# Row-wise max-norm of an 8192 x 8192 matrix: an earlier table load, smaller GpSimd shares and another queue for the last store

## The chip, the cores and the metric

The kernel runs on one core of one Trainium2 chip. Its time is the device time of an execution in microseconds (us). The span in a profile is about 1.8 us shorter than the time of the same execution (627.7 against 629.47 us). Two per cent is 12.6 us.

## The reference

```python
def setup_inputs():
    return {"x": np.random.randn(8192, 8192).astype(np.float32)}

def reference(x):
    return np.linalg.norm(x, ord=np.inf, axis=1)
```

With `axis=1` this is the largest absolute value of each row: 268.4 MB are read, 32 KB are written.

## The kernel before

Rows go to the 128 partitions in 64 tiles of 128 rows. Two single-row tiles come first, then 30 tiles with two rows in each partition, then two single-row tiles, the last of them in five pieces. VectorE reduces nearly everything. In the last three tiles GpSimd takes a share g of the columns. Its reduction takes no absolute value in this kernel, so ScalarE takes that first, in place.

```python
TILES = (                      # pieces of each tile: (columns, columns of GpSimd's share)
    [[(8192, 0)]] * HEAD
    + [[(16384, 0)]] * (PAIRS - 1)
    + [[(16384, 7168)], [(8192, 3584)]]
    + [[(4160, 1792), (2048, 896), (1024, 448), (512, 0), (448, 0)]]
)
...
    def absmax_pool(dst, src):
        keep(nc.scalar.activation(src, src, mybir.ActivationFunctionType.Abs))   # L77
        max_pool(dst, src)                                                       # L66, GpSimd
...
            nc.sync.dma_start(out=buf, in_=src[:, off : off + w])                # L120
            off += w
            if final:
                pairs_out()                     # two transposes, copies and a store on ScalarE
                absmax(res[:, R - 1 :], last)   # L59: the last piece and the partial maxima
            elif u == len(TILES) - 1:
                ...                             # absmax and absmax_pool into columns of `last`
...
    ps_ones = psum_pool.tile([n_ones, P], FP32)
    sb_ones = single.tile([n_ones, P], FP32)
    nc.tensor.transpose(ps_ones, res[:, X_ONE:], ident)
    nc.vector.tensor_copy(out=sb_ones, in_=ps_ones)
    nc.sync.dma_start(out=out[X_ONE * P :].rearrange("(r p) -> r p", p=P), in_=sb_ones)
```

The ring holds three pair tiles; each load waits until VectorE has read what it overwrites (before: 29 such waits of SyncE, 490.8 us in all).

Of the kernel before, what the change touches and what calls it, by code (L numbers as in the profile page):

```python
# [1 line left out]

# [5 lines left out]

P = 128
FP32 = mybir.dt.float32  # L10
INT32 = mybir.dt.int32
MAX = mybir.AluOpType.max
X = mybir.AxisListType.X





HEAD = 2
PAIRS = 30  # L20
TILES = (
    [[(8192, 0)]] * HEAD
    + [[(16384, 0)]] * (PAIRS - 1)
    + [[(16384, 7168)], [(8192, 3584)]]
    + [[(4160, 1792), (2048, 896), (1024, 448), (512, 0), (448, 0)]]
)
RING = 3 * 16384


@with_exitstack  # L30
def kernel(
    ctx: ExitStack,
    tc: tile.TileContext,
    x: bass.AP,
    out: bass.AP,
):
    nc = tc.nc
    n_rows, n_cols = x.shape
    R = n_rows // P
    assert R == 64 and n_cols == 8192  # L40

    X_ONE = 2 * PAIRS
    n_ones = R - X_ONE
    keep = tc.keep_in_program_order

    single = ctx.enter_context(tc.tile_pool(name="single", bufs=1))
    psum_pool = ctx.enter_context(tc.tile_pool(name="psum", bufs=1, space=bass.MemoryType.PSUM))

    ring = single.tile([P, RING], FP32)
    res = single.tile([P, R], FP32)  # L50
    ident = single.tile([P, P], FP32)


    n_part_last = sum((w > g) + (g > 0) for w, g in TILES[-1][:-1])
    w_last = TILES[-1][-1][0]
    last = single.tile([P, w_last + n_part_last], FP32)

    def absmax(dst, src):
        return keep(nc.vector.tensor_reduce(  # L59
            out=dst, in_=src, axis=X, op=MAX, apply_absolute_value=True,  # L60
        )).ins

    def max_pool(dst, src):

        pool = nc.gpsimd
        keep(pool.add_instruction(  # L66
            mybir.InstTensorReduce(
                name=nc.get_next_instruction_name(),
                ins=[pool.lower_ap(src.bitcast(INT32))],
                outs=[pool.lower_ap(dst.bitcast(INT32))],  # L70
                op=MAX,
                axis=X,
            )
        ))

    def absmax_pool(dst, src):
        keep(nc.scalar.activation(src, src, mybir.ActivationFunctionType.Abs))  # L77
        max_pool(dst, src)

    def setup(after):  # L80

        tc.add_manual_dep(
            nc.gpsimd.memset(ident, 0.0).ins, after.name,  # L83
            mybir.DependencyInfo(mybir.DependencyClass.Sync, mybir.DependencyReason.DATA),
            reason="not before the first row is in",
        )
        make_identity(nc, ident, nomemset=True)

    def pairs_out():
        sb = single.tile([PAIRS, P, 2], FP32, name="sb_pairs")  # L90
        both = res[:, :X_ONE].rearrange("p (g r) -> p g r", r=2)
        for r in range(2):
            ps = psum_pool.tile([PAIRS, P], FP32, name=f"ps_pairs{r}")
            nc.tensor.transpose(ps, both[:, :, r], ident)  # L94
            keep(nc.scalar.copy(sb[:, :, r], ps))  # L95
        keep(nc.scalar.dma_start(
            out=out[: X_ONE * P].rearrange("(g p r) -> g p r", p=P, r=2), in_=sb
        ))

    at = 0  # L100
    next_pair, next_one = 0, X_ONE
    for u, pieces in enumerate(TILES):
        k = sum(w for w, _ in pieces) // n_cols
        if k == 2:
            row, next_pair = next_pair, next_pair + 2
        else:
            row, next_one = next_one, next_one + 1
        src = x[row * P : (row + k) * P].rearrange("(p r) m -> p (r m)", r=k)
        off = 0
        n_part = 0  # L110
        for h, (w, g) in enumerate(pieces):
            final = u == len(TILES) - 1 and h == len(pieces) - 1
            if final:
                buf = last[:, :w]
            else:
                if at + w > RING:
                    at = 0
                buf = ring[:, at : at + w]
                at += w
            nc.sync.dma_start(out=buf, in_=src[:, off : off + w])  # L120
            off += w
            if final:
                pairs_out()
                absmax(res[:, R - 1 :], last)
            elif u == len(TILES) - 1:
                for eng, a, e in ((absmax, 0, w - g), (absmax_pool, w - g, w)):
                    if a < e:
                        i = w_last + n_part
                        eng(last[:, i : i + 1], buf[:, a:e])
                        n_part += 1  # L130
            elif g == 0:
                red = absmax(
                    res[:, row : row + k], buf.rearrange("p (c m) -> p c m", m=n_cols)
                )
                if u == 0:
                    setup(red)
            else:

                part = single.tile([P, 2], FP32, name=f"part{u}")
                c = w // n_cols - 1  # L140
                if c:
                    absmax(res[:, row : row + c], buf[:, : c * n_cols])
                absmax(part[:, 0:1], buf[:, c * n_cols : w - g])
                absmax_pool(part[:, 1:2], buf[:, w - g :])
                max_pool(res[:, row + c : row + c + 1], part)

    ps_ones = psum_pool.tile([n_ones, P], FP32)
    sb_ones = single.tile([n_ones, P], FP32)
    nc.tensor.transpose(ps_ones, res[:, X_ONE:], ident)  # L149
    nc.vector.tensor_copy(out=sb_ones, in_=ps_ones)  # L150
    nc.sync.dma_start(out=out[X_ONE * P :].rearrange("(r p) -> r p", p=P), in_=sb_ones)


# [1 line left out]
_INS = ['x']  # L155
_OUTS = [((8192,), 'float32')]


# [23 lines left out]
```

## Time and profile before

| | before |
|---|---|
| time, median of 3 runs | 629.39 us (629.32 to 629.58) |
| span | 627.7 us |
| last pair tile landed | 603.52 us |
| last reduction starts | 624.00 us |
| last store is issued | 625.40 us |
| from that issue to the span's end | 2.30 us |

The page rounds a span to 0.1 us, which is too coarse for what follows; times from a moment to the span's end are taken from the trace files, which have it to 0.001 us. T0 is the start of the VectorE reduction that waits for the last two-row tile. Up to T0 the transfers set the pace: those of x take 99.0% of the span of the 16 DMA engines together, and VectorE idles 2.12 us before the reduction at T0. After it come 24.18 us in which the last tiles are reduced and written. I will count moments of the tail from T0, because T0 itself differs from run to run.

These are the entries of the program's closing line in SyncE's queue (min/median/max duration in ns, then the first and the last start in us):

```profile
L177 SPq EVENT_SEMAPHORE  x7: 17/28/28, 625.8 to 627.6; - x7
L177 SPq DRAIN  x3: 7/7/124, 626.7 to 627.4; - x3
```

One of the three drains takes 124 ns, where the others take 7, and it starts only at 627.4 us.

### The profile page before, as it was taken

How to read it: one execution, taken by the hardware profiler on the slowest of the kernel's cores; microseconds unless marked ns; L12 is line 12 of the kernel's file. 1: busy time of each engine (PE TensorE's matmuls, PEld its weight loads, DVE VectorE, ACT ScalarE, POOL GpSimd, SP SyncE). 2: the span in 40 equal slices, each digit the busy share in tenths (PEclk: the TensorE clock that was granted, in tenths of full speed). 3: DMA queues.
4: the chain of work that ended last, by engine and by line, in shares of the span. 5: the costliest groups of instructions: out<-in, count | busy, mean ns of one | idle time of the engine just before them, and what ended most of it. 6: DMA issues, size and time to landing. Idle time of an engine off the chain costs nothing.

```text
span 627.7 us, 194 instructions
## 1 busy us (share of the span) xinstructions
PE 1.1 (0%) x3; PEld 0.3 (0%) x3; DVE 537.5 (86%) x40; ACT 14.2 (2%) x8; POOL 13.4 (2%) x13
## 2 busy tenths in 40 slices
PE   0000000000000000000000000000000000000000
PEld 0000000000000000000000000000000000000000
DVE  1938988889988889888898888988889988889887
ACT  0000000000000000000000000000000000000044
POOL 0000000000000000000000000000000000000007
DMA  8999999999999999999999999999999999999996
GB/s 368 434 468 401 468 401 468 401 468 401 468 401 468 401 468 401 464 405 464 405 464 405 459 409 459 409 459 409 459 409 451 418 451 418 434 434 422 447 401 269
DMA packets 5525, 268.47 MB, mean 428 GB/s; under 512 B 627, under 2 KB 789, under 8 KB 1045
## 3 DMA queue, kind: packets, MB, share of 16 engines
q1 hardware_dynamic: 5480, 268.44, 99.0%
q10 hardware_dynamic: 45, 0.03, 0.0%
HBM read 268.44 MB, written 0.03 MB: 428 GB/s over the span
## 4 chain that ended last, share of the span: by engine, by line
DMA 70%; DVE 28%; issue 1%; POOL 1%; SPq 0%; POOLq 0%; PE 0%
DMA ring<-in_x_dram 70%; DVE res L59 28%; POOL part L66 0%; POOL last L66 0%; SPq L120 0%; POOLq L177 0%; PE ps_ones L149 0%; DVE sb_ones L150 0%; POOL res L66 0%; POOLq L66 0%
## 5 line engine op out<-in xcount | busy, mean ns | idle before, releaser
L59 DVE TENSOR_REDUCE res<-ring 128x2 f32<-128x16384 f32 (+1 forms) x32 | 525.4, 16420 | 86.8 <-DMA ring<-in_x_dram 86.8
L66 POOL TENSOR_REDUCE part<-ring 128x1 int32<-128x7168 int32 (+1 forms) x2 | 9.3, 4672 | 588.5 <-ACT ring L77 588.5
L77 ACT ACT_TABLE_LOAD x1 | 1.3, 1283 | 603.6 <-DMA ring<-in_x_dram 603.6
L77 ACT ACTIVATE ring<-ring 128x7168 f32<-128x7168 f32 (+4 forms) x5 | 12.6, 2518 | 5.2 <-DMA ring<-in_x_dram 2.9
L59 DVE TENSOR_REDUCE part<-ring 128x1 f32<-128x1024 f32 (+1 forms) x2 | 6.1, 3076 | 0.0
L59 DVE TENSOR_REDUCE last<-ring 128x1 f32<-128x2368 f32 (+3 forms) x4 | 5.2, 1348 | 0.0
L66 POOL TENSOR_REDUCE last<-ring 128x1 int32<-128x1792 int32 (+2 forms) x3 | 3.1, 1061 | 0.0
L94 PE MATMUL ps_pairs<-ident,res 128*30 128x128 f32 x2 | 0.8, 384 | 617.2 <-DVE res L59 612.3
L59 DVE TENSOR_REDUCE res<-last 128x1 f32<-128x455 f32 x1 | 0.6, 628 | 0.6 <-POOL last L66 0.6
L150 DVE COPY sb_ones<-ps_ones 4x128 f32<-4x128 f32 x1 | 0.3, 279 | 0.5 <-PE ps_ones L149 0.5
L83 POOL MEMSET ident<- 128x128 f32 x1 | 0.2, 205 | 21.6 <-DVE res L59 21.6
L94 PEld LDWEIGHTS ps_pairs<-ident,res 128*30 128x30 f32 x2 | 0.2, 106 | 617.5 <-issue 612.3
L95 ACT COPY sb_pairs<-ps_pairs 30x128 f32<-30x128 f32 x2 | 0.4, 254 | 0.0
L66 POOL TENSOR_REDUCE res<-part 128x1 int32<-128x2 int32 x2 | 0.4, 196 | 0.1
L149 PE MATMUL ps_ones<-ident,res 128*4 128x128 f32 x1 | 0.4, 372 | 6.7 <-DVE res L59 6.7
masks.py:199 POOL TENSOR_SCALAR_AFFINE_SELECT ident<-ident 128x128 f32<-128x128 f32 x1 | 0.3, 294 | 0.1
L166 POOL MEMSET const-float32-0.0<- 128x1 f32 x1 | 0.1, 99 | 0.2 <-issue 0.2
L166 POOL MEMSET const-bfloat16-1.0<- 128x1 bf16 x1 | 0.1, 102 | 0.0
L166 POOL MEMSET const-uint8-127<- 128x1 uint8 x1 | 0.1, 102 | 0.0
L166 POOL MEMSET const-float32-1.0<- 128x1 f32 x1 | 0.1, 99 | 0.0
L149 PEld LDWEIGHTS ps_ones<-ident,res 128*4 128x4 f32 x1 | 0.1, 81 | 7.0 <-DVE res L59 7.0
## 6 DMA issues: line engine op xcount, KB each, us to landing
ring<-in_x_dram SPq DMA_DIRECT2D x3, 4096.0 KB, 21.8
ring<-in_x_dram SPq DMA_DIRECT2D x1, 2080.0 KB, 35.7
ring<-in_x_dram SPq DMA_DIRECT2D x1, 1024.0 KB, 37.8
ring<-in_x_dram SPq DMA_DIRECT2D x1, 512.0 KB, 38.6
ring<-in_x_dram SPq DMA_DIRECT2D x30, 40.8
ring<-in_x_dram SPq DMA_DIRECT2D x1, 256.0 KB, 38.8
last<-in_x_dram SPq DMA_DIRECT2D x1, 224.0 KB, 38.8
out_dram<-sb_pairs ACTq DMA_DIRECT2D x1, 30.0 KB, 1.5
```

Of the source, the lines that this page charges most:

```text
L59: return keep(nc.vector.tensor_reduce(out=dst, in_=src, axis=X, op=MAX, apply_absolute_value=True,)).ins
L66: keep(pool.add_instruction(mybir.InstTensorReduce(name=nc.get_next_instruction_name(), ins=[pool.lower_ap(src.bitcast(INT32))], outs=[poo ...
L77: keep(nc.scalar.activation(src, src, mybir.ActivationFunctionType.Abs))
L83: nc.gpsimd.memset(ident, 0.0).ins, after.name,
L94: nc.tensor.transpose(ps, both[:, :, r], ident)
L95: keep(nc.scalar.copy(sb[:, :, r], ps))
L149: nc.tensor.transpose(ps_ones, res[:, X_ONE:], ident)
L150: nc.vector.tensor_copy(out=sb_ones, in_=ps_ones)
L166: nc = _bacc.Bacc("TRN2", target_bir_lowering=False, num_devices=1)
```

## The change

ScalarE loads its table while nothing waits for it; GpSimd gets fewer columns and the last tile is cut a little differently; ScalarE makes the last copy and issues the last store.

```diff
-    + [[(16384, 7168)], [(8192, 3584)]]
-    + [[(4160, 1792), (2048, 896), (1024, 448), (512, 0), (448, 0)]]
+    + [[(16384, 7168)], [(8192, 3328)]]
+    + [[(4160, 1760), (2080, 832), (1024, 384), (512, 0), (416, 0)]]
...
+    def load_table(after):
+        abs_ident = nc.scalar.activation(
+            ident[:, :1], ident[:, :1], mybir.ActivationFunctionType.Abs
+        )
+        tc.add_manual_dep(keep(abs_ident).ins, after.name, ...)
...
                 if u == 0:
                     setup(red)
+                elif u == 1:
+                    load_table(red)
...
-    nc.vector.tensor_copy(out=sb_ones, in_=ps_ones)
-    nc.sync.dma_start(out=out[X_ONE * P :].rearrange("(r p) -> r p", p=P), in_=sb_ones)
+    keep(nc.scalar.copy(sb_ones, ps_ones))
+    keep(nc.scalar.dma_start(
+        out=out[X_ONE * P :].rearrange("(r p) -> r p", p=P), in_=sb_ones
+    ))
```

Cut here: the two transposes of the pair rows move to an earlier place in the program; they still wait for the same data.

More of the change, by code (lines that the diff above doesn't have):

```diff
@@ L87, in setup, with transpose_pairs @@
         make_identity(nc, ident, nomemset=True)
+    def load_table(after):
+        abs_ident = nc.scalar.activation(
+            ident[:, :1], ident[:, :1], mybir.ActivationFunctionType.Abs
+        )
+        tc.add_manual_dep(
+            keep(abs_ident).ins, after.name,
+            mybir.DependencyInfo(mybir.DependencyClass.Sync, mybir.DependencyReason.DATA),
+            reason="not before the second row is in",
+        )
+    ps_pairs = [psum_pool.tile([PAIRS, P], FP32, name=f"ps_pairs{r}") for r in range(2)]
+    def transpose_pairs():
+        both = res[:, :X_ONE].rearrange("p (g r) -> p g r", r=2)
+        for r in range(2):
+            keep(nc.tensor.transpose(ps_pairs[r], both[:, :, r], ident))
     def pairs_out():
         sb = single.tile([PAIRS, P, 2], FP32, name="sb_pairs")
-        both = res[:, :X_ONE].rearrange("p (g r) -> p g r", r=2)
         for r in range(2):
-            ps = psum_pool.tile([PAIRS, P], FP32, name=f"ps_pairs{r}")
-            nc.tensor.transpose(ps, both[:, :, r], ident)
-            keep(nc.scalar.copy(sb[:, :, r], ps))
+            keep(nc.scalar.copy(sb[:, :, r], ps_pairs[r]))
         keep(nc.scalar.dma_start(
@@ L121 @@
             off += w
+            if u == len(TILES) - 1 and h == 0:
+                transpose_pairs()
             if final:
```

## The prediction

> **What bounds the kernel now.** I read the page's engine shares and its slices first. VectorE is busy 86% and nothing else computes before the last 25 us, but the transfers are busy in every slice:
>
> ```profile
> PE 1.1 (0%) x3; PEld 0.3 (0%) x3; DVE 537.5 (86%) x40; ACT 14.2 (2%) x8; POOL 13.4 (2%) x13
> ...
> DMA  8999999999999999999999999999999999999996
> ...
> q1 hardware_dynamic: 5480, 268.44, 99.0%
> ```
>
> The 268.44 MB of x occupy the 16 DMA engines for 99.0% of the span. VectorE takes 17.22 us for a pair tile and then idles 2.12 to 2.14 us for the next one. So the kernel is bound by the stream of x up to about 603 us, and the change leaves that stream as it is: same tiles, same order, same queue, and the same 8192 columns in the last row. What is in play is how long after the stream the program ends.
>
> I then read the chain that ended last, in order of time, from 611 us:
>
> ```profile
> 611.13 2.25 POOL part L66
> ...
> 620.90 1.16 POOL last L66
> 622.06 0.47 issue
> 622.52 0.94 POOL last L66
> 623.46 0.52 POOLq L177
> 623.98 0.02 issue
> 624.00 0.64 DVE res L59
> 624.64 0.04 issue
> 624.68 0.39 PE ps_ones L149
> 625.07 0.02 issue
> 625.09 0.28 DVE sb_ones L150
> ```
>
> The tail runs through GpSimd, then one VectorE reduction, a transpose, a copy and a store. The timeline says why GpSimd is late (columns: start us, duration us, engine, line, operation, count, and in brackets the idle time before it with what ended it):
>
> ```profile
> 603.52 8.69 DVE L59 TENSOR_REDUCE res<-ring 128x1 f32<-128x8192 f32 x1 [2.12 <-DMA ring<-in_x_dram]
> 603.59 1.28 ACT L77 ACT_TABLE_LOAD   x1 [603.59 <-DMA ring<-in_x_dram]
> 604.88 6.18 ACT L77 ACTIVATE ring<-ring 128x7168 f32<-128x7168 f32 x1
> 611.13 6.16 POOL L66 TENSOR_REDUCE part<-ring 128x1 int32<-128x7168 int32 x1 [588.52 <-ACT ring L77]
> 613.25 4.94 DVE L59 TENSOR_REDUCE part<-ring 128x1 f32<-128x4608 f32 x1
> 618.20 1.70 ACT L77 ACTIVATE ring<-ring 128x1792 f32<-128x1792 f32 x1 [1.73 <-DMA ring<-in_x_dram]
> 618.21 5.18 DVE L59 TENSOR_REDUCE last<-ring 128x1 f32<-128x2368 f32 x4
> 624.00 0.63 DVE L59 TENSOR_REDUCE res<-last 128x1 f32<-128x455 f32 x1 [0.61 <-POOL last L66]
> ```
>
> ScalarE gets its first data at about 603.5 us, spends 1.28 us on its table, and only then takes the absolute values that GpSimd needs. From 611.13 GpSimd runs with hardly a gap until 623.98. VectorE is just as unbroken: from 603.52 to 618.21 + 5.18 = 623.39. It then idles 0.61 us for GpSimd. **GpSimd holds the end by 0.61 us, and VectorE is right behind it.** The pieces themselves land at about 618.2, 620.7, 622.0, 622.7 and 623.1 us (issue plus time to landing; where ScalarE waits for them its starts agree), so data are the third bound.
>
> [...] The trace has 1283 ns exactly; the activation follows 1.29 us after the load started[...] and I count 1.28 us. [...] (8686 - 4944) ns / (8192 - 4608) = 1.044 ns an element, at every width. [...] VectorE's 8192 took 8.69 us alone at 23.00 us and 8.69 us beside the rest. So no second-order gain of VectorE from smaller GpSimd shares is counted. [...] No run yet shows the same store from both.
>
> **The change part by part.**
>
> *Table.* An Abs on one column of the identity after row tile 1 pulls the load to about 31.7 us, where ScalarE is idle. Adds one tiny activation off the path; removes 1.28 us before the 7168-wide Abs. Abs 603.60 to 609.78, GpSimd starts at 609.84 instead of 611.13.
>
> *GpSimd's chain.* Its cost is (6163 - 3182) ns / 3584 = 0.832 ns an element, ScalarE's (6176 - 3190) / 3584 = 0.833. GpSimd: 7168 to 616.00, combine to 616.24, 3328 (3.182 - 256 x 0.832 ns = 2.97 us) to about 619.4, combine to 619.6. Now it waits for ScalarE: Abs of 1760 from 618.20, 1.67 us, 619.87; GpSimd 1.66 us to 621.60. The 2080 piece lands 32 columns (16 KB, 0.04 us) later: Abs of 832 620.76 to 621.66, GpSimd 0.88 us to 622.60. Abs of 384 622.08 to 622.60, GpSimd 0.51 us to **623.16**, instead of 623.98. GpSimd becomes bound by landings and gains 0.82 us.
>
> *VectorE's chain.* It receives what GpSimd gives up: +256 columns (8192 piece), then +32, +96 and +64; the last reduction has 416 + 7 = 423 elements instead of 455. Successive reductions start 0.09 us before the former ends (618.21 to 620.74 for a 2.62 us one). 4864 wide: 4.944 + 0.267 = 5.21, from 613.25 to 618.46. 2400 wide: 2.65, from 618.37. 1248 wide: 1.44, from 620.94. 640 wide: 0.82, from 622.30. 512 wide: 0.68, from 623.04 to 623.71. So VectorE's pieces end 0.32 us later than before (623.39), and **VectorE takes over the end from GpSimd** with some 0.55 us to spare. The final reduction reads partial results that VectorE itself has just written; it has a semaphore wait of VectorE's queue ahead of it (0.233 us, begun at 623.2, ended about 0.04 us after the reduction before), so I don't let it overlap: it starts at about 623.77 and takes 0.628 - 32 x 1.044 ns = 0.595, ending at 624.37 against 624.63. Gain 0.26 us: 0.23 from the start, 0.03 from the width.
>
> *Transposes of the pairs.* Moved earlier in program order only. They waited for data (612.35 for VectorE, 617.62 for GpSimd's combine); the second now comes at about 616.3. Nobody on the path reads them. Zero.
>
> *Last copy and store.* The copy goes from VectorE (279 ns) to ScalarE (254 ns mean at 30x128): -0.03 us. The hand-over gains nothing: VectorE's copy ends at 625.37 and SyncE issues at 625.40; ScalarE's own copy to its own issue also took about 0.03 (622.93 to 622.96). The issue took 352 ns on SyncE for four partitions and 632 ns on ScalarE for thirty. After the issue's end both landed alike (1.5 - 0.63 = 0.87 and, by SyncE's wait that ended at 626.65, 1.25 - 0.35 = 0.90 us). I can't split 632 into the engine and the shape, so I put 0.40 on ScalarE: +0.05 us, and up to +0.28. ScalarE's queue is free by then (pairs' issue ends at 623.7).
>
> Sum: -0.26 - 0.03 + 0.05 = **-0.24 us**, so 629.39 - 0.24 = 629.15 us.
>
> **The rivals.** (a) *The saving on GpSimd is had in full:* 0.82 + 0.03 us, some 628.5. Against it: VectorE ended only 0.61 us earlier and receives 448 columns before the final reduction, so this needs work that VectorE can't hide. (b) *ScalarE's store eats it:* if every issue there costs 0.63 us the sum is about -0.01, 629.4. For it: the one issue seen there; against it: that one has 30 partitions. (c) *GpSimd still ends last:* would need a slip of over 0.55 us, for instance if its starts wait on something I don't see; then 629.2 to 629.5. (d) *The stream moves:* a table load or an Abs among the first tiles can't hold back a buffer, since the loads wait for VectorE's reductions and the earlier loads (SyncE's waits name only these), so I count nothing; but the stream's own scatter (runs 629.32 to 629.58) is as large as the effect.
>
> **Range and chances.** From -0.6 us (half way to (a), a lucky store) to +0.15 us (b plus scatter): 628.8 to 629.55. Two per cent are 12.6 us, while the whole tail after the stream, from 623.1 us to the span's end at 627.7, is 4.6 us. Removing it all would not be "faster", and nothing added is near 12 us. Faster 0.01, same 0.98, slower 0.01.
>
> **What would show it.** Right: the table load near 31.7 us; GpSimd's first big reduction at 609.8; the last reduction idle for VectorE's own result, not for GpSimd, with a start near 623.77 counted from the same landing of 603.5; GpSimd done 0.5 us before; the chain of waits with VectorE in place of GpSimd; ScalarE's last issue at 0.35 to 0.45 us. Wrong: a GpSimd wait left before the last reduction, a last issue of 0.6 us, or landings of the last pieces that moved by more than 0.1 us, which would mean the stream and not the tail made the difference.

The 1283 ns are the table load, and 1.044 ns an element is VectorE's reduction ((17220 - 8686) / 8192 and (8686 - 628) / (8192 - 455) both give 1.042). That smaller GpSimd shares bring VectorE no further gain rests on the two times of 8.69 us alone. The 0.04 us for 16 KB are an estimate; at the page's mean of 428 GB/s they come to 0.038.

## The result

The changed kernel took 628.66 us (median of 6 runs, 628.54 to 628.75), the kernel before beside it 629.36 us (629.15 to 629.63). The ratio is 0.9988, with a 95% interval from 0.9976 to 1.0001. A ratio is the mean time of one kernel's fast runs over that of the other's of the same rounds, so not quite the ratio of these medians. All outputs are right. The class (within 2%) was right, but the time fell below the predicted range of 628.8 to 629.55.

The timeline of the changed kernel, for the lines that were shown of before (start, duration, engine, line, operation, idle time before it and what ended it):

```profile
31.39 1.28 ACT L91 ACT_TABLE_LOAD   x1 [31.39 <-DVE res L59]
...
603.17 8.69 DVE L59 TENSOR_REDUCE res<-ring 128x1 f32<-128x8192 f32 x1 [2.14 <-DMA ring<-in_x_dram]
603.25 6.18 ACT L77 ACTIVATE ring<-ring 128x7168 f32<-128x7168 f32 x1 [570.36 <-DMA ring<-in_x_dram]
609.50 6.16 POOL L66 TENSOR_REDUCE part<-ring 128x1 int32<-128x7168 int32 x1 [587.26 <-ACT ring L77]
...
618.03 5.32 DVE L59 TENSOR_REDUCE last<-ring 128x1 f32<-128x2400 f32 x4
619.61 3.10 POOL L66 TENSOR_REDUCE last<-ring 128x1 int32<-128x1760 int32 x3 [0.39 <-ACT ring L77]
...
623.44 0.59 DVE L59 TENSOR_REDUCE res<-last 128x1 f32<-128x423 f32 x1
...
624.50 0.26 ACT L169 COPY sb_ones<-ps_ones 4x128 f32<-4x128 f32 x1 [2.06 <-PE ps_ones L168]
624.79 0.26 ACTq L170 DMA_DIRECT2D out_dram<-sb_ones  x1
```

The table load is out of the way (it takes 1.28 us from 31.39, and the activation behind it starts 1.30 us after it, at 32.69; before it was 1.29 us, 603.59 to 604.88), and GpSimd starts 6.33 us after T0 instead of 7.61. GpSimd is done at 619.61 + 3.10 = 622.71 us, VectorE's pieces only at 618.03 + 5.32 = 623.35. The last reduction no longer names a wait for GpSimd. The chain that ended last, in order of time, agrees: from T0 to the transpose it is VectorE alone.

```profile
603.17 8.69 DVE res L59
611.86 6.25 DVE part L59 x2
618.11 5.25 DVE last L59 x4
623.36 0.04 DVEq L59
623.39 0.05 issue
623.44 0.60 DVE res L59
```

From T0 the last reduction starts at 623.44 - 603.17 = 20.27 us (before: 20.48) and the last issue at 21.62 (before: 21.88). So the tail up to the issue is 0.26 us shorter. But from the issue to the span's end it is 2.00 us instead of 2.30. That is 0.30 us that the prediction did not have. The closing entries of SyncE's queue show a difference there; the late drain is gone:

```profile
L198 SPq EVENT_SEMAPHORE  x6: 17/28/28, 622.2 to 626.7; - x6
L198 SPq DRAIN  x3: 7/7/7, 626.0 to 626.3; - x3
```

The rest of the difference between the two profiles is T0 itself, 603.17 against 603.52 us, and it was there from the very first tile (landed at 12.92 against 13.30 us), where the two kernels do the same.

### The profile page after: what moved, and what is told of

Read it like the earlier page. It is cut to its first block, busy times and chain, and to the rows that moved or that the text cites. A ratio compares the mean times of both kernels' runs of the same rounds, so it can differ in the third digit from the quotient of the medians.

```text
span 626.8 us, 194 instructions
## 1 busy us (share of the span) xinstructions
PE 1.1 (0%) x3; PEld 0.3 (0%) x3; DVE 537.5 (86%) x39; ACT 14.3 (2%) x10; POOL 13.3 (2%) x13
## 4 chain that ended last, share of the span: by engine, by line
DMA 70%; DVE 29%; issue 0%; PE 0%; SPq 0%; ACT 0%; DVEq 0%
DMA ring<-in_x_dram 70%; DVE res L59 28%; DVE part L59 1%; DVE last L59 1%; PE ps_ones L168 0%; SPq L135 0%; ACT sb_ones L169 0%; DVEq L59 0%
## 5 line engine op out<-in xcount | busy, mean ns | idle before, releaser
L59 DVE TENSOR_REDUCE last<-ring 128x1 f32<-128x2400 f32 (+3 forms) x4 | 5.3, 1392 | 0.0
L66 POOL TENSOR_REDUCE last<-ring 128x1 int32<-128x1760 int32 (+2 forms) x3 | 3.0, 1016 | 0.5 <-ACT ring L77 0.4
L91 ACT ACT_TABLE_LOAD x1 | 1.3, 1283 | 31.4 <-DVE res L59 31.4
```

Of the source, the lines that this page charges most:

```text
L59: return keep(nc.vector.tensor_reduce(out=dst, in_=src, axis=X, op=MAX, apply_absolute_value=True,)).ins
L66: keep(pool.add_instruction(mybir.InstTensorReduce(name=nc.get_next_instruction_name(), ins=[pool.lower_ap(src.bitcast(INT32))], outs=[poo ...
L91: abs_ident = nc.scalar.activation(ident[:, :1], ident[:, :1], mybir.ActivationFunctionType.Abs)
```

## The experiments

The theory after the result had three terms: the tail up to the last issue, the end after it, and a scatter of T0. The rivals: the early table load makes the first tiles land sooner; or one part of the change carries all. Fourteen experiments ran, two of them repeats of the kernels before and after. All numbers of the tail come from one profile each, counted from that profile's T0. The last column is the median of all runs of the kernel in its batch.

| kernel | T0 | last reduction starts after T0 | last issue to end | T0 to end | time, median |
|---|---|---|---|---|---|
| before | 603.52 | 20.48 | 2.30 | 24.18 | 629.36 |
| before, again | 603.22 | 20.49 | 2.30 | 24.19 | 629.18 |
| table only | 603.10 | 19.92 | 2.30 | 23.62 | 628.71 |
| shares and recut only | 603.59 | 20.27 | 2.29 | 23.93 | 629.07 |
| copy and store only | 603.10 | 20.49 | 2.01 | 23.87 | 628.96 |
| changed | 603.17 | 20.27 | 2.00 | 23.62 | 628.66 |
| changed, again | 603.15 | 20.27 | 2.00 | 23.61 | 628.64 |
| changed, old shares | 603.25 | 19.92 | 2.00 | 23.31 | 628.27 |
| changed, old copy and store | 603.17 | 20.27 | 2.29 | 23.93 | 628.97 |
| changed, old store | 603.66 | 20.27 | 2.07 | 23.68 | 628.79 |
| changed, old copy | 603.21 | 20.28 | 2.00 | 23.65 | 628.76 |

Here the time less "T0 to end" lies between 604.96 and 605.18 us. So the tail explains most of the differences between the times, and some 0.2 us is scatter that it doesn't.

### One part at a time, on the kernel before

**Only the table.**

```diff
                 if u == 0:
                     setup(red)
+                elif u == 1:
+                    load_table(red)
```

> Only the early table load, on the kernel before. Theory (three separate terms: a tail term that either the table or the recut alone gives, a store term, and a first-landing term that is scatter): GpSimd's first big reduction starts 6.25 us after the last pair tile landed instead of 7.6, its pieces end near 623.2 on the old clock, VectorE's at 623.4 set the end, so the last reduction starts about 0.55 us sooner after that landing; time 0.5 us below before, some 628.85. First landing of x anywhere between 12.9 and 13.3 us. Rival (the early table load itself makes the first rows land sooner): first landing at 12.9 us again and 0.85 us below before, some 628.5.

628.71 us, ratio 0.9991 (0.9979 to 1.0004). The last reduction starts 0.56 us sooner after T0 than before: more than in the whole change. The timeline shows VectorE at its old pieces, without the wait for GpSimd:

```profile
617.78 5.14 DVE L59 TENSOR_REDUCE last<-ring 128x1 f32<-128x2368 f32 x4
...
619.55 3.22 POOL L66 TENSOR_REDUCE last<-ring 128x1 int32<-128x1792 int32 x3
...
623.02 0.63 DVE L59 TENSOR_REDUCE res<-last 128x1 f32<-128x455 f32 x1
```

**Only the shares and the recut.**

```diff
-    + [[(16384, 7168)], [(8192, 3584)]]
-    + [[(4160, 1792), (2048, 896), (1024, 448), (512, 0), (448, 0)]]
+    + [[(16384, 7168)], [(8192, 3328)]]
+    + [[(4160, 1760), (2080, 832), (1024, 384), (512, 0), (416, 0)]]
```

> Only the smaller GpSimd shares and recut last pieces. Theory: GpSimd ends near 623.55 and VectorE near 623.7 on the old clock, so the last reduction starts 0.2 us sooner after the landing of the last pair tile, and is 0.03 us shorter: the same 0.23 to 0.26 us that the whole change shows in its tail, without the table; time some 629.1. Rival (the table is what the tail gains from, the shares only follow): no gain here, 629.36.

629.07 us, ratio 0.9997 (0.9984 to 1.0009). The last reduction starts 20.27 us after T0, exactly as in the whole change, although the table load still sits in the path and GpSimd starts 7.62 us after T0. So with these shares the early table adds nothing: VectorE's extra columns set the end either way. The two transposes stand at their old place here, so moving them changed nothing either.

**Only the copy and the store.**

```diff
-    nc.vector.tensor_copy(out=sb_ones, in_=ps_ones)
-    nc.sync.dma_start(out=..., in_=sb_ones)
+    keep(nc.scalar.copy(sb_ones, ps_ones))
+    keep(nc.scalar.dma_start(out=..., in_=sb_ones))
```

> Only the last copy and store on ScalarE. Theory: tail up to the last reduction unchanged; from the start of the last issue to the span's end 2.0 us instead of 2.3, because the issue takes 0.26 instead of 0.35 us and SyncE's last drain no longer holds the closing barrier; time 0.3 us below before, 629.05. Rival (the store's place is neutral and the 0.3 us were chance): 629.36, 2.3 us from issue to the end.

628.96 us, ratio 0.9995 (0.9982 to 1.0007). The last reduction still waits for GpSimd (0.66 us), and from the last issue to the end it is 2.01 us. The 0.29 us at the end are real and belong to this part.

**The kernel before, again.**

> The kernel before, unchanged, for a second profile. Theory: the first landing of x (13.30 us before, 12.92 after the change) scatters from run to run, so it may come anywhere from 12.9 to 13.3 here; ratio 1.000 within 0.0003. Rival (the change moved it): 13.3 us again, in this and in every kernel without an early table load.

629.18 us, ratio 0.9998 (0.9985 to 1.0012). The first tile landed at 12.94 us this time, T0 was 603.22, and the tail was 24.19 us. Over all profiles the first landing lay between 12.87 and 13.30 us and T0 between 603.10 and 603.98, with and without an early table load. So the 0.35 us between the first two T0 need no cause in the change; they are within this scatter.

### One part undone, in the changed kernel

**Old shares and pieces, with the early table and the new store.** The edit is the second one above, backwards.

> The changed kernel with the shares and last pieces of before. Theory: with the table early, the recut costs what VectorE has to do more: VectorE's pieces end 0.3 us sooner than in the changed kernel, GpSimd's near the same moment as VectorE's; time 0.25 to 0.3 us below the changed kernel, some 628.4. Rival (the recut carries part of the gain): 628.7 or above.

628.27 us (628.23 to 628.37), ratio 0.9985 (0.9972 to 0.9997). This is the fastest median of all, and the only interval that leaves out 1. VectorE's pieces end 0.35 us sooner than in the changed kernel. The recut costs what it gives VectorE to do.

**Old copy and old store.** The edit is the third one, backwards.

> The changed kernel with the last copy on VectorE and the last store on SyncE again. Theory: 0.3 us above the changed kernel, some 628.95, with 2.3 us from the last issue to the span's end and a late drain of SyncE in it. Rival (the store's place is neutral): equal to the changed kernel, 628.66.

628.97 us, ratio 0.9997 (0.9983 to 1.0010): 0.3 us above the changed kernel of the same batch, 2.29 us from issue to end, and the late drain is back:

```profile
L196 SPq DRAIN  x3: 7/7/124, 626.1 to 626.8; - x3
```

**Copy on ScalarE, store on SyncE.**

```diff
     keep(nc.scalar.copy(sb_ones, ps_ones))
-    keep(nc.scalar.dma_start(out=..., in_=sb_ones))
+    nc.sync.dma_start(out=..., in_=sb_ones)
```

> The changed kernel with the copy on ScalarE but the store on SyncE. Theory: the copy's engine is worth 0.02 to 0.03 us and the queue the rest, so this is 0.25 to 0.3 us above the changed kernel and within 0.05 of the version with both undone. Rival (it is the copy and store on the same engine that gains, or the copy): near the changed kernel.

This was a miss. 628.79 us, ratio 0.9994 (0.9981 to 1.0006), and from the issue to the end 2.07 us, though SyncE issues the store, in 0.34 us. No drain is late:

```profile
L196 SPq DRAIN  x3: 7/7/7, 626.6 to 626.9; - x3
```

So most of the 0.3 us came without the queue; 0.07 us went with it.

**The changed kernel, again.**

> The changed kernel once more, the yardstick of this batch: 628.66, ratio to before 0.9988; its last reduction 20.27 us after the last pair tile landed. The first landing may differ from 12.92 us if it is scatter; if the change had moved it, 12.9 us again.

628.64 us, ratio 0.9991 (0.9979 to 1.0004), tail as before.

### What the late drain depends on

So far SyncE's last drain was late in every kernel with VectorE's copy and SyncE's store, and in no other. But these kernels also had more instructions in SyncE's program. Counted in the traces (waits, transfers and drains together), SyncE has 81 recorded instructions in all of them, 80 with the copy moved, and 78 in the changed kernel. With VectorE's copy the closing line of SyncE has one wait more (seven instead of six). The new theory: the delay depends on the length of SyncE's program, not on who copies or stores. The rival: it is VectorE's copy.

**One load less, with old copy and old store.**

```diff
-    + [[(4160, 1760), (2080, 832), (1024, 384), (512, 0), (416, 0)]]
+    + [[(4160, 1760), (2080, 832), (1024, 384), (928, 0)]]
```

> Copy on VectorE and store on SyncE again, but the last two pieces of 512 and 416 columns joined into one of 928, so SyncE's program has one load less: 80 recorded instructions or fewer. Theory (length of SyncE's program): drain of 0.007 us and 2.03 us from the last issue to the end, although VectorE copies and SyncE stores; the last reduction ends about 20.8 us after the last pair tile landed, time near 628.6. Rival (VectorE's copy or SyncE's store delays the close): 2.28 us and a drain of 0.12.

80 recorded instructions, 2.13 us from issue to end, and no late drain, with VectorE copying and SyncE storing:

```profile
L196 SPq DRAIN  x3: 7/7/7, 626.2 to 626.6; - x3
```

628.79 us, ratio 0.9993 (0.9979 to 1.0007). The last reduction ended 20.81 us after T0. The expected 2.03 us were missed by 0.1: here two closing waits instead of one follow the landing of the store, 0.06 us apart, and SyncE's last wait is late (see below).

**Old copy, new store.**

```diff
-    keep(nc.scalar.copy(sb_ones, ps_ones))
+    nc.vector.tensor_copy(out=sb_ones, in_=ps_ones)
```

> The changed kernel with the copy on VectorE and the store on ScalarE. Theory (length of SyncE's program: it has no store here, 78 or 79 recorded instructions): 2.03 us from issue to end; the copy takes 0.28 instead of 0.25 us, so 0.03 us above the changed kernel at most. Rival (VectorE's copy delays the close): 2.28 us.

628.76 us, ratio 0.9992 (0.9979 to 1.0006), 79 recorded instructions, 2.00 us from issue to end. VectorE's copy alone delays nothing. It took 0.28 us against 0.26. The runs also price the queue. ScalarE's issue of this store took 0.26 to 0.27 us, SyncE's 0.34 to 0.35. But from the start of the issue to the wait of SyncE that the landing ends it was 1.18 to 1.19 us with ScalarE and 1.21 to 1.22 with SyncE, so only 0.02 to 0.04 us of the shorter issue arrived there.

**One more wait for SyncE, first attempt.** In the version with ScalarE's copy and SyncE's store, the load of tile 10 also waits for the activation that loaded the table.

> Copy on ScalarE and store on SyncE, as in the run that lost only part of the gain, plus one more wait in SyncE's program (the load of one early pair tile also waits for the activation that loaded the table, long done). SyncE then has 81 recorded instructions, as in every kernel whose last drain of SyncE took 0.12 us and came 0.3 us late; the version without the extra wait has 80 and a drain of 0.007. Theory (the late drain depends on how many instructions SyncE's program has, not on who copies or stores): 2.28 us from the last issue to the span's end, with a drain of 0.12 us. Rival (it is VectorE's copy, or the wait of SyncE on VectorE, that delays the close): 2.03 us, drain 0.007.

628.80 us, ratio 0.9993 (0.9978 to 1.0008), 2.08 us from issue to end. This run decides nothing: no instruction was added, and the trace counts 80 as before.

**One more wait, second attempt.** The same load also waits for a small memset that GpSimd makes after the third tile. Now a wait instruction is added, and 80 become 81. The edit is shown in part, against the version with ScalarE's copy and SyncE's store; the memset and its wait are cut.

```diff
-            nc.sync.dma_start(out=buf, in_=src[:, off : off + w])
+            load = nc.sync.dma_start(out=buf, in_=src[:, off : off + w])
+            if u == 10:
+                for one in one_more:     # the table's activation, the memset
+                    tc.add_manual_dep(load.ins, one.name, ...)
```

> Copy on ScalarE and store on SyncE, with the load of one early pair tile waiting for two more, long finished instructions, so that SyncE's program gets one more wait instruction (81 recorded instead of 80). Theory (length of SyncE's program): the last drain of SyncE takes 0.12 us again and the time from the last issue to the span's end is 2.28 us instead of 2.03. Rival (it is what copies and stores at the end): 2.03 us and a drain of 0.007.

629.17 us, ratio 0.9997 (0.9981 to 1.0014), 2.31 us from issue to end, and the drain is late again, with ScalarE copying:

```profile
L215 SPq DRAIN  x3: 7/7/124, 626.5 to 627.2; - x3
```

The added wait was passed at 156.4 us, some 470 us before the end, so it cannot hold up the end by its waiting. Making the program one instruction longer brought the late drain, and making it one shorter took it away.

**The same two waits, with old copy and old store (82).**

> Copy on VectorE and store on SyncE, with the same two waits: 82 recorded instructions of SyncE instead of 81. Theory (something happens when SyncE reaches a certain instruction of its program, so a longer program meets it one instruction earlier): the delay is still there, 2.2 to 2.35 us from issue to end, but it may show at another instruction than the last drain. Rival (one exact length): drain of 0.007 and 2.05 us.

628.95 us, ratio 0.9996 (0.9981 to 1.0011), 2.13 us from issue to end. This falls between the two expectations. The drain takes 13 ns. The wait just before it is now late, at 627.4 us, where the other engines pass the same wait at 627.1:

```profile
L215 SPq EVENT_SEMAPHORE  x1: 17/17/17, 627.4 to 627.4; - x1
```

So the delay has moved one instruction earlier, as a fixed place in a program that got one longer would. There most of it lies beside GpSimd's closing work, which also ended at 627.4 us.

The trace files show this in every run. Count SyncE's recorded instructions from the first: the 80th starts 0.46 to 0.47 us after the 79th in all ten profiles that have an 80th, whatever it is.

| recorded instructions of SyncE | profiles | the 80th is | usual gap before such an entry | store's landing to span's end |
|---|---|---|---|---|
| 78 or 79 | 6 | none | | 0.81 to 0.82 us |
| 80 | 3 | the last wait, which also waits for the other engines | 0.38 us | 0.86 to 0.91 us |
| 81 | 6 | the last drain | 0.09 us | 1.08 to 1.09 us |
| 82 | 1 | the wait before the last drain | 0.15 us | 0.91 us |

So the delay was not absent with 80: it fell on the last wait, where 0.07 us of it stood out. The place is fixed in SyncE's program in these ten profiles, and what the delay costs depends on what lies there. What causes the delay at this place was not shown by any run.

### A little more for GpSimd

**Old shares, but 3712 instead of 3584 of the 8192 piece.**

```diff
-    + [[(16384, 7168)], [(8192, 3584)]]
+    + [[(16384, 7168)], [(8192, 3712)]]
```

> The best version so far (table early, store on ScalarE, shares of before) with GpSimd's share of the 8192 piece raised from 3584 to 3712. Theory (with the table early VectorE is the bound there by some 0.15 us): VectorE's pieces end 0.13 us sooner, at 19.70 us after the last pair tile landed, GpSimd's at 19.75; last reduction at 19.8 instead of 19.93; time 0.1 us below the version with 3584, 628.2, which may drown in the scatter. Rival (GpSimd ends last again, for every column given to it costs as much): last reduction at 19.95 or later.

628.42 us (628.29 to 629.23), ratio 0.9990 (0.9977 to 1.0002); the last reduction starts 19.93 us after T0, not sooner than with 3584. Neither expectation was right:

```profile
617.90 5.14 DVE L59 TENSOR_REDUCE last<-ring 128x1 f32<-128x2368 f32 x4 [0.16 <-DMA ring<-in_x_dram]
```

VectorE, relieved by 0.13 us, idles 0.16 us for the next piece to land. With the old shares the landing of this piece paces it already.

## Why the prediction was wrong

**The bound and the take-over: right.** The prediction had GpSimd's end at 623.16, VectorE's pieces at 623.71, the last reduction at 623.77 and its end at 624.37. Counted from its T0 of 603.52 these are 19.64, 20.19, 20.25 and 20.85 us. Measured were 19.54, 20.18, 20.27 and 20.86. The step that VectorE takes over is shown, and so is the gain that it leaves: 0.24 us at the end of the last reduction, where 0.26 were predicted. One check in it was weak: the 8192-wide reduction that ran "beside the rest" met GpSimd for only 1.08 of its 8.69 us (611.13 to 612.21). The conclusion stands all the same: from the widths 16384 and 8192, which ran mostly without GpSimd, the 4608 columns come to 4.95 us, and beside GpSimd they took 4.94.

**Which part gives it: not asked.** The prediction let the table's 1.28 us and the smaller shares work together and did not work out either alone. Either is enough to take GpSimd off the end (table only: 0.56 us sooner; recut only: 0.21), and together they give only the smaller gain, because the recut loads VectorE. Working out two half changes would have shown this from the same numbers.

**The copy: right.** 0.256 us on ScalarE against 0.279 on VectorE.

**The last store: the step that failed.** The prediction put "0.40 on ScalarE: +0.05 us, and up to +0.28". It held everything after the issue fixed except for the issue's own length. Measured: 2.00 us instead of 2.30 from the start of the issue to the end, a gain of 0.30 us where a loss of 0.05 stood. The issue was the smaller miss: it took 0.26 us on ScalarE, not 0.40, against 0.35 on SyncE, and the landing came 0.04 us sooner after its start (1.18 against 1.22). The larger one is the stretch from the landing to the span's end, which the prediction took for a constant (627.7 - 626.65 = 1.05 us by its figures): counted from the start of SyncE's wait for the landing, it went from 1.08 to 0.82 us. These 0.26 us are the late drain, which went away because SyncE's program got shorter. The prediction did not read the closing entries, where the drain of 124 ns stood out.

**The remainder.** The tails differ by 24.18 - 23.62 = 0.56 us, the medians by 0.70 in the first comparison and 0.60 in the second. The rest is within the scatter before T0. The tail's gain alone, 629.36 - 0.56 = 628.80 us, would have lain on the edge of the range, so part of the distance is scatter.

**The rivals.** Rival (a), GpSimd's saving in full, had named some 628.5 us. The time came close to it, but for another reason: GpSimd's saving was not had in full. Rivals (b), ScalarE's store as a cost, and (c), GpSimd still last, fell. Rival (d), the stream, was right only as scatter.

## What to carry to other kernels

When two engines end as close to each other as here (VectorE idled 0.61 us for GpSimd), relieve one and load the other only after working out each half alone: here the early table with the old shares was the better kernel (628.27 against 628.64 us beside it). Read the closing entries of the queues as carefully as the chain that ended last, since an engine that does no work can hold the end: here SyncE's late drain cost 0.26 us. Count a tail from a fixed event inside the trace, so that a scatter of 0.4 us in the stream does not pass for a gain. And do not subtract from a span rounded to 0.1 us when hundredths are asked: here that hid 0.07 us between two runs.
